# Dilated attention heads of an encoder layer: values two tiles later, and values, transposes and scores in that order within a step

## The chip, the cores and the metric

The kernel runs on one core of one Trainium2 chip. Its metric is the device time of one execution in microseconds (us). A core has five engines that work side by side, each through its own list of instructions in order: TensorE (PE in the profile; its weight loads, which can overlap its matmuls, are listed as PEld), VectorE (DVE), ScalarE (ACT), GpSimd (POOL) and SyncE (SP), which here only issues transfers (DMAs). Engines wait for one another by semaphores. TensorE writes into PSUM, which is cut into banks of 512 float32 values for each of 128 partitions; VectorE and ScalarE read it and write SBUF.

## What is computed

One encoder layer with two attention branches, gates, and an MLP, for a sample of 1024 positions and a prompt of 256. The part that the change touches is the second branch, twelve heads in three groups with dilations 1, 4 and 16:

```python
B_GROUPS = ((128, 1), (512, 4), (2048, 16))
B_HEADS_PER_GROUP = 4

def _dilated_mixture(q, k, v, bias_b):
    for gi, (window, dil) in enumerate(B_GROUPS):
        o, lse = _banded_attention(_to_residues(q[:, :, hs], dil), _to_residues(k[:, :, hs], dil),
                                   _to_residues(v[:, :, hs], dil), window // (2 * dil), dil,
                                   bias_b[:, hs], None)
        ...
    alpha = jax.nn.softmax(jnp.stack(lses), axis=0)
    o = jnp.sum(alpha[..., None] * jnp.stack(outs).astype(jnp.float32), axis=0)
```

Within a head: scores q k^T plus a bias, a maximum over the row, the exponential, its sum, and the product with v. The rest of the layer is `h = rmsnorm(x)`, `z = h @ w_in`, gated sums of the two branches, and `x + square(relu(h @ w_up)) @ w_down`.

## The kernel before

Positions lie in ten tiles of 128. The kernel goes through stages: values of v and the norm; the product with `w_in` in 14 pairs of column blocks; the windowed heads with the remaining gate columns; the merge and `w_out`; the MLP. Each float32 product is made from three products of rounded parts (`hi`, `lo`), and the large ones by a scheme that trades one of eight block products for sums; so each weight block is split on ScalarE (`hi`, L316) and VectorE (`lo`, L318) before use.

The dilated heads run inside the product with `w_in`, in the last five column pairs (`MIXED` = 9 to 13). `pair` (L950) makes one pair with blocks of dense matmuls (`seven`, `prompt`) and calls `tick` (L1015) in the middle of each block and after it. Every second tick advances the generator `attention_b` (L482) by one step. So a step of the heads lands in the middle of each dense block, and twelve dense matmuls of 512 columns (or twenty-four of 256) stand between two steps on TensorE. The schedule is written by hand: the program's order is each engine's order.

`tick` also calls `flush` (L858), which issues stores of gate columns (`scr_g`) on SyncE that were queued two or more ticks before, ahead of the step of that tick. With the last five pairs `right_pair` (L374) issues its two weight loads (512 KB each, `raw`) on SyncE once in a pair, after the block `S2`, and then advances a split by one operation at a time: ScalarE's part, VectorE's part, and the sums of the block scheme on VectorE.

`attention_b` has 60 tiles of two heads each: for each of two pairs of heads, ten tiles of group 2, ten of group 1 and ten of group 0. A *flat* tile has 128 keys (W = 128), a *band* tile 256 keys, a *split* tile two halves of 64 queries with 128 keys each. Group 2 is flat; group 1 alternates band and split, then has two flat ones; group 0 has seven bands, a split, a band and a split. A step handles tiles j and j + 1 for even j:

- `load_v(j)` (L503): v of a tile from DRAM on SyncE, 64 KB for each block of 128 keys, four buffers.
- `load(j)` (L491): q and k of a tile on SyncE (`qk`, four buffers), and at the first tile of a group its bias on GpSimd.
- `scores(j)` (L512): score matmuls of tiles j and j + 1 into two `sc` banks, one for each head, then on VectorE the sum with the bias into `s` with the row maximum (L533) and its negative into `o` (L535). A head has 64 values, so these matmuls use 64 of the 128 rows. A float32 matmul here is two instructions.
- `exponentials(j)` (L538): two exponentials on ScalarE, in place in `s`.
- `transposes(j, eng)` (L546): two or four transposes of `s` into a `pt` bank (two of these), and a copy by `eng` into the tile's half of `turned_s`.
- `values_of(j, eng, pv)` (L558): value matmuls into the tile's quarter of the `pv` bank (one buffer), a copy by `eng` into `o`, and the store of `o` on GpSimd's queue.

In step j these stand in this order, which is the one each engine's list gets: `load_v` of j - 1 and j; scores of j and j + 1; `load` of j + 4 and j + 5; transposes of j - 2 (copied by ScalarE); values of j - 3 (copied by ScalarE); exponentials of j and j + 1; transposes of j - 1 (copied by VectorE); values of j - 2 (copied by VectorE). So an even tile's values follow its own transposes within a step, and an odd tile's follow in the next. There are 32 steps.

Of the kernel before, what the change touches and what calls it, by code (L numbers as in the profile page):

```python
# [15 lines left out]
P = 128  # L16
# [6 lines left out]
HD = 64  # L23
# [6 lines left out]
ROW = 2 * HD + 4  # L30
# [67 lines left out]
def encoder_kernel(  # L98
# [5 lines left out]
    nc = tc.nc  # L104
# [31 lines left out]
    def bank(tag, name=None):  # L136
        return psum.tile([P, 512], F32, name=name or tag, tag=tag, bufs={"mm": 3, "sc": 2, "pt": 2, "pv": 1}[tag])
# [130 lines left out]
    def moved(eng, out, in_):  # L268

        if eng is nc.scalar:  # L270
            nc.scalar.activation(out, in_, AF.Copy)  # L271
        else:
            nc.vector.tensor_copy(out, in_)
# [208 lines left out]
    def attention_b(make):  # L482
# [3 lines left out]
        order = [(g, i, t, tile) for i in range(2) for g in (2, 1, 0) for t, tile in enumerate(_group_tiles(g))]  # L486
        n = len(order)
        held, live, bias = {}, {}, {}
# [14 lines left out]
        def load_v(j):  # L503
            if not 0 <= j < n:
                return
            g, i, t, (pieces, W, _) = order[j]
            v = held[j][1] = make("v", (P, 2, P), n=4)
            for a, (_, _, _, ka) in enumerate(pieces):
                for k in range(W // P):
                    nc.sync.dma_start(v[:, a + k, :], values_rows(g, i, ka // P + k))  # L510

        def scores(j):  # L512

            banks = [bank("sc") for _ in range(2)]
            at = lambda k, h: banks[h][:, 2 * P * (k - j) : 2 * P * (k - j) + order[k][3][1]]
            for k in (j, j + 1):
                g, i, t, (pieces, W, c0) = order[k]
                qk = held[k][0]
                for h in range(2):
                    rows = HALVES[h]  # L520
                    for a, (p0, nq, _, _) in enumerate(pieces):
                        nc.tensor.matmul(at(k, h)[p0 : p0 + nq, :], qk[rows, p0 : p0 + nq],  # L522
                                         qk[rows, P + P * a : P + P * a + W], start=True, stop=True,
                                         skip_group_check=True)
            for k in (j, j + 1):
                g, i, t, (pieces, W, c0) = order[k]
                whole, *flat = bias[g, i]
                b = whole[:, :, c0 : c0 + W] if c0 is not None else flat[pieces[0][2] >= NS]
                s = make("s", (P, 2, 2 * P), n=4)
                m = small.tile([P, 2], F32, name="m", tag="m")  # L530
                o = make("o", (P, ROW), n=5)
                for h in range(2):
                    nc.vector.tensor_tensor_reduce(s[:, h, :W], at(k, h), b[:, h, :], 1.0, -3.0e38,  # L533
                                                   op0=ALU.add, op1=ALU.max, accum_out=m[:, h : h + 1])
                nc.vector.tensor_scalar(o[:, 2 * HD : 2 * HD + 2], m, -1.0, None, op0=ALU.mult)  # L535
                live[k] = s, o
# [18 lines left out]
            moved(eng, pt[:, :a, :], ps[:, : P * a].rearrange("p (i q) -> p i q", q=P))  # L555
            live[j] = pt, o

        def values_of(j, eng, whole):  # L558

            if not 0 <= j < n:  # L560
                return
            g, i, t, (pieces, W, _) = order[j]
            (pt, o), (_, v) = live.pop(j), held.pop(j)
            pv = whole[:, P * (j % 2) : P * (j % 2) + P]
            for h in range(2):
                for a, (p0, nq, _, _) in enumerate(pieces):
                    for k in range(W // P):
                        nc.tensor.matmul(pv[p0 : p0 + nq, HD * h : HD * h + HD], pt[:, 2 * k + h, p0 : p0 + nq],  # L568
                                         v[:, a + k, HALVES[h]], start=k == 0, stop=k == W // P - 1,
                                         skip_group_check=True)  # L570
            moved(eng, o[:, : 2 * HD], pv)
            for p0, nq, qa, _ in pieces:
                nc.gpsimd.dma_start(scr_b[g][qa : qa + nq, i, :], o[p0 : p0 + nq, :])

# [4 lines left out]
        load(3)  # L579
        yield  # L580
        yield
        for j in range(0, n + 3, 2):
            load_v(j - 1)
            load_v(j)
            if j < n:
                scores(j)
            load(j + 4)
            load(j + 5)
            pv = bank("pv") if j else None
            if 0 < j <= n:  # L590
                transposes(j - 2, nc.scalar)
            values_of(j - 3, nc.scalar, pv)
            if j < n:
                exponentials(j)
                exponentials(j + 1)
            if 0 < j <= n:
                transposes(j - 1, nc.vector)
            values_of(j - 2, nc.vector, pv)
            yield

    def entering():
# [443 lines left out]
    if True:  # L1045
# [11 lines left out]
        live, units = {}, {}  # L1057
# [139 lines left out]
    if True:  # L1197
# [61 lines left out]
        order = [(u, t) for u in range(4) for t in range(NT)]  # L1259
        n = len(order)  # L1260
# [277 lines left out]
    class Down:  # L1538
# [4 lines left out]
        def make(self, name, shape=(P, 2, 512), dt=F32):  # L1543
            return self.late.tile(list(shape), dt, name=name, tag="l4", bufs=8)
# [334 lines left out]
```

## Time and profile before

| | us |
|---|---|
| time, median of 3 runs | 1748.45 |
| lowest and highest run | 1746.77, 1752.15 |
| span of the profiled execution | 1745.6 |
| first scores of the dilated heads, after the start of the span | 358.5 |
| last values of the dilated heads | 543.4 |

The profile is of one execution; the page gives the span of that execution and no time of its own beside it, so what lies around the span isn't seen apart from the runs: their median is 2.85 us above the span. A row of a list in order of time has the start, the duration, the engine, the line of the kernel, the operation, the result and its inputs, the shape and a count; `[0.38 <-ACT o L271]` behind it says that the engine sat idle for 0.38 us before it and that ScalarE's instruction on `o` at line 271 released it. Where the engine that is named had long been done, the true releaser is another one, often a transfer. A row with a count above one stands for several instructions in a run. The end of a matmul is modelled: matmuls overlap, so the distance between two starts says more than a duration. SPq rows are issues of transfers on SyncE; the list of transfers gives for each kind its size and the time from issue to landing.

### The profile page before, as it was taken

What the parts mean: (1) busy time and instruction counts of PE and PEld (TensorE: products, weight loads), DVE (VectorE), ACT (ScalarE), POOL (GpSimd) and SP (SyncE); (2) the same over time, 40 slices, a digit from 0 to 9 for tenths busy, and PEclk for the clock granted to TensorE, in tenths of its full rate; (3) what the DMA queues carried; (4) which work ended last, traced back from release to release, by engine and by line L of the source; (5) the groups of instructions that cost most, each with busy time, mean ns of one, the idle gap of its engine ahead of it and who ended that gap; (6) DMA issues with size and microseconds to landing.
All of it is one profiled execution on the core that took longest, in us unless ns stands there. A gap on an engine that the chain in (4) does not pass through costs nothing.

```text
span 1745.6 us, 25270 instructions
## 1 busy us (share of the span) xinstructions
PE 1713.3 (98%) x9248; PEld 1453.1 (83%) x9248; DVE 976.1 (56%) x1708; ACT 725.4 (42%) x1528; POOL 521.0 (30%) x452
## 2 busy tenths in 40 slices
PE   7999999999999999999999999999999999999998
PEld 6898888877778899988888788888888788888886
DVE  6732323445553566676558645454546776657575
ACT  6232222355553455654346433333333333333344
POOL 0212222212221344200000255555655442304050
PEclk9999999999999999999999999999999999999999
DMA  6414343566555753476212243344336844633333
GB/s 235 143 43 151 101 135 115 143 189 174 166 156 151 216 169 82 125 273 219 71 48 97 85 154 124 118 144 154 124 123 239 296 160 151 217 115 115 115 115 121
DMA packets 214780, 256.36 MB, mean 147 GB/s; under 512 B 24887, under 2 KB 144523, under 8 KB 214528
## 3 DMA queue, kind: packets, MB, share of 16 engines
q1 hardware_dynamic: 201424, 228.26, 40.5%
q0 software_dynamic: 12144, 24.38, 4.6%
q10 hardware_dynamic: 1088, 2.10, 0.3%
q8 instruction: 73, 1.20, 0.3%
q14 instruction: 51, 0.42, 0.1%
HBM read 169.10 MB, written 90.73 MB: 149 GB/s over the span
## 4 chain that ended last, share of the span: by engine, by line
PE 88%; DVE 4%; ACT 3%; DMA 2%; issue 2%; POOL 1%; SPq 0%; ACTq 0%; DVEq 0%; POOLq 0%
PE dn L351 20%; PE x L351 17%; PE mm L192 13%; PE z L351 9%; PE v L735 5%; PE pv L351 5%; PE mm L351 4%; PE y L351 4%; PE pv L1104 2%; PE pv L568 2%; PE sc L522 1%; PE pt L1091 1%; PE pt L553 1%; PE tr L342 1%; PE sc L1067 1%
## 5 line engine op out<-in xcount | busy, mean ns | idle before, releaser
L351 PE MATMUL dn<-dhi,ulo 128*128 128x512 f32 x448 | 174.6, 390 | 2.7 <-DVE ulo L186 2.7
L351 PE MATMUL dn<-dhi,uhi 128*128 128x512 f32 x448 | 174.3, 389 | 0.0
L351 PE MATMUL dn<-dlo,uhi 128*128 128x512 f32 x448 | 174.3, 389 | 0.0
L351 PE MATMUL x<-chi,wlo 128*128 128x512 f32 x424 | 167.3, 394 | 2.1 <-DVE u L1752 1.4
L351 PE MATMUL x<-clo,whi 128*128 128x512 f32 x424 | 165.7, 391 | 0.1
L351 PE MATMUL x<-chi,whi 128*128 128x512 f32 x424 | 165.1, 389 | 0.0
L318 DVE TENSOR_TENSOR wlo<-ta,whi 128x1024 fp32r<-128x1024 f32 x30 | 55.8, 1858 | 178.4 <-ACT whi L316 178.4
L318 DVE TENSOR_TENSOR wlo<-raw,whi 128x1024 fp32r<-128x1024 f32 x60 | 90.7, 1512 | 95.3 <-ACT whi L316 95.3
L393 POOL TENSOR_TENSOR tb<-raw 128x512 f32<-128x512 f32 x25 | 33.7, 1347 | 362.6 <-PE mm L192 137.6
L351 PEld LDWEIGHTS dn<-dhi,ulo 128*128 128x128 f32 x448 | 84.1, 188 | 21.3 <-DVE ulo L186 3.8
L186 DVE TENSOR_TENSOR ulo<-uraw,uhi 128x1024 fp32r<-128x1024 f32 x56 | 92.9, 1679 | 11.7 <-ACT uhi L185 11.7
L351 PEld LDWEIGHTS dn<-dhi,uhi 128*128 128x128 f32 x448 | 84.1, 188 | 17.5
L351 PEld LDWEIGHTS dn<-dlo,uhi 128*128 128x128 f32 x448 | 84.1, 188 | 17.3
L351 PEld LDWEIGHTS x<-chi,wlo 128*128 128x128 f32 x424 | 79.8, 188 | 18.4 <-issue 1.8
L351 PEld LDWEIGHTS x<-chi,whi 128*128 128x128 f32 x424 | 79.6, 188 | 17.1
L351 PEld LDWEIGHTS x<-clo,whi 128*128 128x128 f32 x424 | 79.8, 188 | 14.9 <-DVE clo L318 0.4
L1577 POOL TENSOR_TENSOR t<-raw,t 128x1024 f32<-128x1024 f32 x16 | 47.8, 3007 | 141.2 <-DMA raw<-in_w_down_dram 141.2
L1728 DVE TENSOR_TENSOR v<-v,dn 128x512 f32<-128x512 f32 x90 | 59.5, 682 | 42.9 <-PE dn L351 38.2
L271 ACT ACTIVATE pt<-pt 128x512 f32<-128x512 f32 (+1 forms) x70 | 39.1, 558 | 91.0 <-PE pt L553 71.7
L1824 POOL TENSOR_TENSOR u<-u,u 128x640 f32<-128x640 f32 x16 | 25.6, 1597 | 163.2 <-ACT u L1749 163.2
L351 PE MATMUL pv<-phi,wlo 128*128 128x256 f32 x256 | 72.5, 283 | 1.7 <-ACT u L1748 1.7
L351 PE MATMUL dn<-dhi,up 128*128 128x512 f32 x224 | 73.5, 389 | 0.0
(337 smaller groups left out, 4801.4 us busy)
## 6 DMA issues: line engine op xcount, KB each, us to landing
scr_u<-u SPq DMA_DIRECT2D x112, 320.0 KB, 2.6
uraw<-scr_u SPq DMA_DIRECT2D x56, 512.0 KB, 4.3
raw<-in_w_in_dram SPq DMA_DIRECT2D x33, 512.0 KB, 5.9
raw<-in_w_up_dram SPq DMA_DIRECT2D x32, 512.0 KB, 5.3
raw<-in_w_down_dram SPq DMA_DIRECT2D x28, 512.0 KB, 6.7
sg<-scr_g SPq DMA_DIRECT2D x32, 256.0 KB, 5.1
uraw<-scr_u SPq DMA_DIRECT2D x28, 256.0 KB, 4.6
v<-scr_v SPq DMA_DIRECT2D x96, 64.0 KB, 2.4
```

What stands on the lines that cost most here:

```text
L186: nc.vector.tensor_tensor(lo, src, hi.bitcast(F32), op=ALU.subtract)
L192: nc.tensor.matmul(ps, a, b, start=i == 0, stop=i == len(seq) - 1)
L271: nc.scalar.activation(out, in_, AF.Copy)
L318: nc.vector.tensor_tensor(lo, src, hi.bitcast(F32), op=ALU.subtract)
L351: nc.tensor.matmul(ps, a, b, start=first and i == 0, stop=last and i == len(seq) - 1, skip_group_check=True)
L393: (nc.vector if vector else nc.gpsimd).tensor_tensor(o, x, y, op=ALU.subtract)
L568: nc.tensor.matmul(pv[p0 : p0 + nq, HD * h : HD * h + HD], pt[:, 2 * k + h, p0 : p0 + nq], v[:, a + k, HALVES[h]], start=k == 0, stop=k == ...
L735: nc.tensor.matmul(ps[:, :n], a, b, start=k == 0 and j == 0, stop=k == KC - 1 and j == 2)
L1104: nc.tensor.matmul(pv[:, HD * h : HD * h + HD], pt[:, 2 * b + h, :], src, start=b == 0, stop=b == W // P - 1)
L1577: nc.gpsimd.tensor_tensor(o, a, b, op=ALU.subtract)
L1728: nc.vector.tensor_tensor(v, v, ps, op=ALU.add)
L1824: nc.gpsimd.tensor_tensor(u[S1], u21, u22, op=ALU.add)
```

## The change

Within a step the order becomes: `load_v` of j - 2 and j - 1; values of j - 4 and j - 3, one behind the other into the `pv` bank; their copies (ScalarE, VectorE) and stores; transposes of j - 2 and j - 1, each with its copy; scores of j and j + 1; `load` of j + 4 and j + 5; exponentials. The copy and the store leave `values_of` for a new function, `store_values`. An even tile's values thus come a whole step after its transposes, as the odd tile's do. `s` gets two buffers instead of four, `o` eight instead of five. The range of steps runs to n + 4 instead of n + 3, which is 32 steps in both.

```diff
--- before.py
+++ after.py
@@ -526,9 +526,9 @@
                 g, i, t, (pieces, W, c0) = order[k]
                 whole, *flat = bias[g, i]
                 b = whole[:, :, c0 : c0 + W] if c0 is not None else flat[pieces[0][2] >= NS]
-                s = make("s", (P, 2, 2 * P), n=4)
+                s = make("s", (P, 2, 2 * P), n=2)
                 m = small.tile([P, 2], F32, name="m", tag="m")
-                o = make("o", (P, ROW), n=5)
+                o = make("o", (P, ROW), n=8)
                 for h in range(2):
                     nc.vector.tensor_tensor_reduce(s[:, h, :W], at(k, h), b[:, h, :], 1.0, -3.0e38,
                                                    op0=ALU.add, op1=ALU.max, accum_out=m[:, h : h + 1])
@@ -555,12 +555,10 @@
             moved(eng, pt[:, :a, :], ps[:, : P * a].rearrange("p (i q) -> p i q", q=P))
             live[j] = pt, o
 
-        def values_of(j, eng, whole):
-
-            if not 0 <= j < n:
-                return
-            g, i, t, (pieces, W, _) = order[j]
-            (pt, o), (_, v) = live.pop(j), held.pop(j)
+        def values_of(j, whole):
+
+            _, _, _, (pieces, W, _) = order[j]
+            pt, v = live[j][0], held.pop(j)[1]
             pv = whole[:, P * (j % 2) : P * (j % 2) + P]
             for h in range(2):
                 for a, (p0, nq, _, _) in enumerate(pieces):
@@ -568,7 +566,11 @@
                         nc.tensor.matmul(pv[p0 : p0 + nq, HD * h : HD * h + HD], pt[:, 2 * k + h, p0 : p0 + nq],
                                          v[:, a + k, HALVES[h]], start=k == 0, stop=k == W // P - 1,
                                          skip_group_check=True)
-            moved(eng, o[:, : 2 * HD], pv)
+
+        def store_values(j, eng, whole):
+            g, i, _, (pieces, _, _) = order[j]
+            o = live.pop(j)[1]
+            moved(eng, o[:, : 2 * HD], whole[:, P * (j % 2) : P * (j % 2) + P])
             for p0, nq, qa, _ in pieces:
                 nc.gpsimd.dma_start(scr_b[g][qa : qa + nq, i, :], o[p0 : p0 + nq, :])
 
@@ -579,23 +581,25 @@
         load(3)
         yield
         yield
-        for j in range(0, n + 3, 2):
+        for j in range(0, n + 4, 2):
+            load_v(j - 2)
             load_v(j - 1)
-            load_v(j)
+            if j > 2:
+                pv = bank("pv")
+                values_of(j - 4, pv)
+                values_of(j - 3, pv)
+                store_values(j - 4, nc.scalar, pv)
+                store_values(j - 3, nc.vector, pv)
+            if 0 < j <= n:
+                transposes(j - 2, nc.scalar)
+                transposes(j - 1, nc.vector)
             if j < n:
                 scores(j)
             load(j + 4)
             load(j + 5)
-            pv = bank("pv") if j else None
-            if 0 < j <= n:
-                transposes(j - 2, nc.scalar)
-            values_of(j - 3, nc.scalar, pv)
             if j < n:
                 exponentials(j)
                 exponentials(j + 1)
-            if 0 < j <= n:
-                transposes(j - 1, nc.vector)
-            values_of(j - 2, nc.vector, pv)
             yield
 
     def entering():
```

## Prediction

> **What bounds the kernel now.** I read the page first, then the busy times by stage, then the waits of the stage that the change touches, then single steps of it in order of time.
>
> ```profile
> span 1745.6 us, 25270 instructions
> ...
> PE 88%; DVE 4%; ACT 3%; DMA 2%; issue 2%; POOL 1%; SPq 0%; ACTq 0%; DVEq 0%; POOLq 0%
> ```
>
> TensorE (PE) carries 88% of the chain that ended last. So a change is worth what it takes from TensorE's own time: cycles between two matmuls in which it has nothing to do. The dilated heads lie in one stage, from the first scores to the last values:
>
> ```profile
> 358.00:545.00 187.00, 182.94 (x1295) 142.70 (x1294) 97.41 (x400) 97.75 (x334) 44.65 (x80) 1.00 0.59 165
> ```
>
> The columns are the stretch, its length, then busy us of PE, PE's weight loads, VectorE, ScalarE and GpSimd, the granted clock, the DMA share and GB/s. PE's modelled busy time hides short waits, since the modelled ends overlap; VectorE and ScalarE are at 52% each (97.4 and 97.8 of 187), so neither is the bound. The clock is 1.00 throughout. The waits of the weight loads in this stage (total us, times, longest) show the thing that the change aims at:
>
> ```profile
> PEld pv L568 <- ACT o L271: 10.1, 29, 0.5
> ...
> PEld pv L568 <- DVE m L533: 1.7, 8, 0.5
> ```
>
> 29 of the 30 steps that have an even tile's values wait there for ScalarE's copy of the odd tile's values out of the same PSUM bank. One step in order of time, with two flat tiles (W = 128), shows it:
>
> ```profile
> 463.08 0.39 PE L351 MATMUL x<-clo,whi 128*128 128x512 f32 x1
> ...
> 463.31 0.39 PE L351 MATMUL x<-chi,whi 128*128 128x512 f32 x1
> ...
> 463.63 0.71 PE L522 MATMUL sc<-qk 64*128 64x128 f32 x8
> ...
> 464.28 0.44 PE L553 MATMUL pt<-ident,s 128*128 128x128 f32 x2
> ...
> 464.38 0.29 DVE L533 CUSTOM_DVE_ANT_0 s<-sc,bias 128x128 f32<-128x128 f32 x1 [0.51 <-PE sc L522]
> ...
> 464.55 0.56 PE L568 MATMUL pv<-v,pt 128*128 128x64 f32 x4
> ...
> 464.95 0.39 PE L553 MATMUL pt<-ident,s 128*128 128x128 f32 x2
> ...
> 465.15 0.28 ACT L271 ACTIVATE o<-pv 128x128 f32<-128x128 f32 x1
> ...
> 465.32 0.39 ACT L543 ACTIVATE s<-s,o 128x128 f32<-128x128 f32 x1
> ...
> 465.47 0.52 PEld L568 LDWEIGHTS pv<-v,pt 128*128 128x128 f32 x4 [0.38 <-ACT o L271]
> ...
> 465.94 0.48 PE L351 MATMUL x<-chi,wlo 128*128 128x512 f32 x1
> ...
> 466.47 0.39 ACT L543 ACTIVATE s<-s,o 128x128 f32<-128x128 f32 x1
> ```
>
> Dense matmuls start every 0.23 us (463.08, 463.31), so the last one is through at 463.54, and the next dense one starts at 465.94: the step costs PE 2.40 us. In it, eight score instructions take 0.65 (463.63 to 464.28), two transposes 0.27, four value matmuls 0.40 (464.55 to 464.95), two transposes about 0.24. That ends at 465.19, but the even tile's values start at 465.47, 0.04 after the copy into o ends (465.15 + 0.28). PE has lost 0.28 us.
>
> **The change, part by part.** Edits are costed on PE's time line.
>
> *1. The wait that goes.* The same reading for a step with a band and a split tile, and for one with two bands:
>
> ```profile
> 448.59 0.44 PE L553 MATMUL pt<-ident,s 128*128 128x128 f32 x2
> 449.19 1.10 PE L568 MATMUL pv<-v,pt 128*128 128x64 f32 x8 [0.17 <-ACT o L271]
> ```
>
> ```profile
> 428.20 1.00 PE L568 MATMUL pv<-v,pt 128*128 128x64 f32 x8
> 429.04 0.61 PE L553 MATMUL pt<-ident,s 128*128 128x128 f32 x4
> 429.57 1.10 PE L568 MATMUL pv<-v,pt 128*128 128x64 f32 x8
> ```
>
> Band and split: two transposes from 448.59 end at about 448.83, values at 449.19: 0.36 lost; such steps differ a little by which tile is the split one, and I take 0.34. Two bands: four transposes (0.49) from 429.04 end at 429.53, values at 429.57: 0.04. The tiling gives 12 flat, 12 band-and-split and 6 band steps: 12 x 0.28 + 12 x 0.34 + 6 x 0.04 = 7.7 us. After the change the values of a step have their transposed probabilities from the step before, and both tiles' values precede both copies, so this wait has no cause left. So does a wait at 368.42 (row in part 4), the longest of the second row of waits, 0.5: there the odd tile's values wait for their v load, and the new order has that wait in part 4. Together **-8.2 us**.
>
> *2. Where the array changes shape.* Scores use 64 of the 128 rows, and their weight loads don't run ahead: 463.31 + 0.23 to 463.63 is 0.09 lost on entering. On leaving:
>
> ```profile
> 359.12 0.50 PE L351 MATMUL x<-chi,wlo 128*128 128x512 f32 x1
> 359.46 0.39 PE L351 MATMUL x<-clo,whi 128*128 128x512 f32 x1
> ```
>
> 0.34 instead of 0.23 to the next dense matmul, 0.11 lost. Now scores are entered from the dense matmuls and left for transposes; after, they are entered from transposes and left for dense ones: still one way in, one way out. The other new border, dense to a full-row float32 instruction, is in the last step, which has no scores:
>
> ```profile
> 537.36 0.40 PE L351 MATMUL z<-hhi,whi 128*128 128x512 f32 x1
> ...
> 537.60 0.60 PE L553 MATMUL pt<-ident,s 128*128 128x128 f32 x4
> ```
>
> 0.24 apart: nothing lost. So 0, within 0.1 us a step either way (30 steps: -3 to +3).
>
> *3. What becomes late: the exponentials.* The reductions wait for a bank that both tiles' scores fill: the first starts at 464.38, 0.10 after the last score instruction, and the first exponential 0.94 later (465.32). After the change the scores are PE's last work of the step, so with T the return to dense matmuls the last exponential ends near T + 0.1 + 0.7 + 1.54 = T + 2.35, against T + 0.92 now (466.47 + 0.39 against 465.94). Their reader, the next transposes, comes after twelve dense matmuls (2.77) and the values (0.80): T + 3.57. Covered by 1.2 us. For two bands an exponential takes 0.50:
>
> ```profile
> 429.41 0.50 ACT L543 ACTIVATE s<-s,o 128x256 f32<-128x256 f32 x1
> ```
>
> Four of them end near T + 3.0, and the values ahead of the transposes take 1.7 (two times 0.84, 428.20 to 429.04): again 1.4 to spare. Cost 0; without this cover it would be about 1 us a step. The copies move ahead of the reductions on VectorE and of the exponentials on ScalarE, where they wait for PE work that is earlier in the step. Weight splits and evacuations queue behind the exponentials and come 1.4 us later; their readers on PE are a whole block of twelve matmuls and a step away, over 4 us.
>
> *4. What becomes late: the v loads.* This is the cost. Values now open a step: the loads that they need are wanted about 1.3 us earlier (scores 0.65, transposes 0.27, the switch 0.2, and the saving), and SyncE, which issues everything in order, holds its qk loads until the scores that free their buffers, now the last PE work: 0.9 us later in a flat step. Behind those stand the raw weight loads, and behind these the v loads. In order of issue, with the landing of the first v behind each pair of weight loads and PE's first values:
>
> ```profile
> 362.07 0.71 PE L522 MATMUL sc<-qk 64*128 64x128 f32 x8
> ```
>
> ```profile
> 360.84 1.15 SPq L381 DMA_DIRECT2D raw<-in_w_in_dram  x2
> 362.04 2.82 SPq L510 DMA_DIRECT2D v<-scr_v  x2
> ```
>
> ```profile
> v<-scr_v SPq DMA_DIRECT2D x1, 64.0 KB, 6.2
> ```
>
> ```profile
> 368.42 0.63 PE L568 MATMUL pv<-v,pt 128*128 128x64 f32 x4 [0.30 <-DVE m L533]
> ```
>
> ```profile
> 464.33 0.38 SPq L498 DMA_DIRECT2D qk<-scr_qb  x1
> ...
> 467.23 1.08 SPq L381 DMA_DIRECT2D raw<-in_w_in_dram  x2
> 468.41 2.35 SPq L510 DMA_DIRECT2D v<-scr_v  x2
> ```
>
> ```profile
> v<-scr_v SPq DMA_DIRECT2D x1, 64.0 KB, 6.0
> ```
>
> ```profile
> DMA to landing us min/median/max: 1.8/2.4/6.2
> ```
>
> A v load takes 2.4 us in the median but 6.2 and 6.0 behind weight loads. *Tiles 0 and 1:* both v loads will stand where the row at 362.04 stands and land from 368.24 on. PE: the step at j = 2 begins at 361.98 (0.09 before 362.07), transposes 0.49, switches 0.2, scores 0.65, dense 2.77: ready at 366.1. It waits 2.1. *Tiles 36 and 37:* the step at j = 36 is the one shown; its dense matmuls end at 463.54, by the saving of the step before at 463.26. PE leaves it at 463.26 + 0.80 + 0.49 + 0.65 + 0.2 = 465.4; qk loads begin at 465.2 instead of 464.33, so the v load is issued at 469.3 instead of 468.41 and lands 6.0 later, at 475.3. PE gets there after dense 2.77, a step of 2.14 and dense 2.77, at 473.1. It waits 2.2. The same working at the two other weight loads, ahead of tiles 18 and 54, gives 0.2 and 0, because band tiles lengthen the steps between.
>
> *5. Gate stores ahead of v loads.* SyncE also waits for a gate sum that VectorE makes behind a weight split:
>
> ```profile
> 458.49 0.68 DVE L927 TENSOR_TENSOR z<-y,c 128x512 f32<-128x512 f32 x1
> ```
>
> ```profile
> 459.20 0.32 SPq L860 DMA_DIRECT2D scr_g<-z  x1
> 459.62 0.88 SPq L510 DMA_DIRECT2D v<-scr_v  x2
> ```
>
> Since the split follows the exponentials, all this slides by 1.4 us: the store to 460.6, the two v loads to 461.0 and 461.5, landing (2.4) by 463.9. Tile 33's values are wanted at 463.26 + 0.40 = 463.7. Some 0.2 to 0.5 here; the places like it are the one-in-nine steps after a split in four column pairs, and the same slide gives 0.4, 0.4, 0.2 and 0.1 at those that matter. Parts 4 and 5 sum to 2.1 + 2.2 + 0.2 + 1.1 = 5.6; bounds: 0 if every v lands in 1.8, and 14 if each of the 24 steps that are not two bands waits 0.4 besides the two long ones.
>
> *6. The rest at nothing.* GpSimd: the stores of o now precede the bias loads of the same step; they wait for copies at most 2 us, and a bias is wanted two steps (about 10 us) later. s with 2 buffers: transposes that free them precede the scores on PE. o with 8: six are live, two are on their way out; that is as much room as now. v and qk keep 4. The number of steps stays 32; the last one gets two tiles' values instead of one, the step at j = 2 loses one.
>
> Sum: -8.2 + 0 + 5.6 = **-2.6 us**. The profiled span is 1745.6, 2.85 under the median of 1748.45; against the median this gives 1745.8.
>
> A sentence beside this from the Trainium skill, *DMA: Bandwidth & Descriptors*, section "Queues, rings and completion order": descriptors of a ring are consumed in ring order; the 6.2 against 2.4 us agrees. By that page's "Specifications" (about 358 GB/s of HBM for a core) the 1.05 MB of two weight loads would take 2.9 us, an estimate, after which v would land near 366 at the first place instead of 368.24; both long waits would be gone and the sum would be about -7. The measured landings decide.
>
> **Rivals.**
>
> *The v loads are never late* (SyncE or the rings have more room than the two rows say). For it: the median of 2.4 us, and most steps have 2 us to spare by the working of part 4. Against it: 368.42, where the present order already waits for a v. Then -8.2: 1740.2.
>
> *The v loads become the bound (slower).* Place: SyncE's queue, where qk loads now wait for the end of the step's PE work, so that each v load starts a step's length behind it. Price: in a flat step v is issued near T + 3.2 and wanted at T + 2.77 + 2.14 + 2.77 = T + 7.7; a landing after more than 4.5 us stalls PE one for one. It decides from 8.2 us of waits in all, 0.27 a step. With 14 us, +5.8: 1754.3. For it: landings of 5 to 6 us in four places; against: they are four.
>
> *The change doesn't do what it says:* the values still wait for a copy, since there is one values bank (pv) and the next step's values need both copies of the last. Against it: those copies are issued before exponentials and are over 2 us old by then. Then 0 + 5.6: 1754.
>
> **How the numbers follow.** The forecast, part of the gain eaten by late v loads, gets 0.50, with its own range 1743 to 1749; never late 0.27; v the bound 0.17; wait stays 0.06. A measurement of this kernel can tell about 0.3%, 5.2 us, from no change, so the forecast itself counts as the same. Faster by more: the 0.27 and 0.04 of the forecast's fast edge, 0.31. Slower by more: most of the two slow rivals, 0.19. Same: 0.50. The range leaves a tenth out on each side: 1739 to 1756.5.
>
> **What would show it.** Right: no wait of pv for o on ScalarE; flat steps of 4.9 instead of 5.2 us; pv waiting for v at tiles 0 and 36 for about 2 us; exponentials ending 2.3 us into the dense matmuls with no wait of the transposes. Wrong: transposes waiting for s (part 3), values waiting for v in most steps, or a gap between scores and dense matmuls above 0.11 (part 2).

## The result, and the profile after

The kernel got slower by 0.28%: 1752.82 us in the median after (1749.2 to 1758.89, 20 runs) against 1747.91 before (1746.48 to 1752.15, 20 runs); the ratio is 1.0028 with a 95% interval of 1.002 to 1.0036. That is 4.9 us, a little less than the 5.2 us that the prediction took as the least it could tell from no change; with 20 runs of each the interval still lies clear of 1. The forecast was 1745.8.

First the page's head and its chain of waits:

```profile
span 1751.8 us, 25171 instructions
...
PE 85%; DVE 5%; DMA 4%; ACT 3%; issue 2%; SPq 1%; POOL 1%; DVEq 0%; ACTq 0%; POOLq 0%
```

The profiled span is 6.2 us longer than before (1751.8 against 1745.6), and 4% of the chain is now DMA, 2% before. The stage of the dilated heads, as before by busy us of PE, its weight loads, VectorE, ScalarE and GpSimd, granted clock, DMA share and GB/s:

```profile
358.00:549.00 191.00, 182.34 (x1294) 149.00 (x1293) 95.39 (x398) 99.50 (x334) 43.78 (x79) 0.97 0.57 162
```

The granted clock is 0.97 where it was 1.00. The first dense matmul behind the stage starts at 547.55 instead of 543.35, and the first scores of the windowed heads follow at 578.60 instead of 574.39: of these 4.2 us, 3.9 are lost in this stage and 0.3 ahead of it. The other 2 us lie behind it: a copy that splits a raw weight (at 594.05, before at 588.53) waits 1.7 us for its load instead of 0.4, and the remaining 0.6 us was not followed up.

The waits of the stage, of PE and of its weight loads (total us, times, longest):

```profile
PE pv L566 <- DMA v<-scr_v: 8.3, 6, 3.5
```

```profile
PEld pv L566 <- issue: 9.0, 6, 3.9
```

The row with ScalarE's copy of o (10.1 us, 29 times) is gone, and no row of the transposes waiting for s has come. In their place PE waits six times for v, 8.3 us in all, once 3.5. These six lie in five steps (j = 4, 18, 28, 40 and 58); shorter waits for v in four others stand under another engine's name or in no row of their own. A row counts from the modelled end of the last dense matmul; by the distance between starts a wait is some 0.16 us longer, and the text below goes by that unless it quotes a row. The second row is the weight loads' side of the same waits: what stands in front of them waits, and they with it. VectorE has a large new row, for which PE doesn't wait:

```profile
DVE o L273 <- ACT o L271: 49.0, 19, 7.4
```

The second tile's copy waits for the first one, which reads the same bank. An undisturbed flat step (the one at j = 8) in order of time, on PE and then on ScalarE:

```profile
377.48 0.39 PE L351 MATMUL x<-chi,whi 128*128 128x512 f32 x1
377.70 1.00 PE L566 MATMUL pv<-v,pt 128*128 128x64 f32 x8
378.54 0.61 PE L553 MATMUL pt<-ident,s 128*128 128x128 f32 x4
379.08 0.71 PE L522 MATMUL sc<-qk 64*128 64x128 f32 x8
379.72 0.50 PE L351 MATMUL x<-chi,wlo 128*128 128x512 f32 x1
```

```profile
378.74 0.28 ACT L271 ACTIVATE o<-pv 128x128 f32<-128x128 f32 x1 [0.39 <-PE pv L566]
...
381.44 0.40 ACT L543 ACTIVATE s<-s,o 128x128 f32<-128x128 f32 x1 [2.09 <-DVE o L535]
...
382.62 0.39 ACT L543 ACTIVATE s<-s,o 128x128 f32<-128x128 f32 x1
```

From 377.71 (the last dense matmul's start and 0.23) to 379.72 the step costs PE 2.01 us, 0.39 less than the flat step shown of before. The last exponential ends at 383.01, 3.3 us into the dense work, and nothing waits for it. And the worst step, at j = 40, whose values need tiles 36 and 37; SyncE's issues first, then the time to landing of that v load, then PE:

```profile
463.24 0.32 SPq L864 DMA_DIRECT2D scr_g<-z  x1
...
464.62 0.39 SPq L498 DMA_DIRECT2D qk<-scr_qb  x1
...
467.44 1.38 SPq L381 DMA_DIRECT2D raw<-in_w_in_dram  x2
468.87 2.42 SPq L510 DMA_DIRECT2D v<-scr_v  x1
```

```profile
v<-scr_v SPq DMA_DIRECT2D x1, 64.0 KB, 6.4
```

```profile
471.47 0.39 PE L351 MATMUL x<-chi,whi 128*128 128x512 f32 x1
475.39 1.94 PE L566 MATMUL pv<-v,pt 128*128 128x64 f32 x8 [3.53 <-DMA v<-scr_v]
...
478.11 1.86 PE L522 MATMUL sc<-qk 64*128 64x256 f32 x12
479.90 0.79 PE L351 MATMUL x<-chi,wlo 128*128 128x512 f32 x1
```

The v load is issued at 468.87 behind 1.05 MB of raw weights and lands 6.4 us later, at 475.27; PE has been ready since 471.70. What the wait costs doesn't end there: eight value matmuls take 1.94 us instead of 1.00, and the scores 1.86 instead of about 1.08 for the same twelve. The same view by windows shows why (the column before the last two is the granted clock):

```profile
473.00:474.00 1.00, 0.00 (x0) 0.00 (x0) 0.00 (x0) 0.00 (x0) 0.00 (x0) 0.90 1.11 309
474.00:475.00 1.00, 0.00 (x0) 0.00 (x0) 0.00 (x0) 0.00 (x0) 0.00 (x0) 0.50 0.82 227
475.00:480.00 5.00, 4.61 (x25) 3.33 (x25) 0.71 (x2) 0.66 (x2) 1.07 (x2) 0.50 0.28 81
480.00:481.00 1.00, 1.00 (x3) 0.84 (x4) 0.93 (x6) 0.00 (x0) 0.00 (x0) 0.69 0.31 81
...
535.00:536.00 1.00, 1.00 (x8) 1.00 (x8) 0.02 (x1) 0.28 (x1) 0.00 (x0) 0.62 0.00 0
536.00:538.00 2.00, 2.00 (x10) 1.02 (x8) 0.69 (x2) 0.60 (x1) 1.07 (x2) 0.50 0.18 63
538.00:539.00 1.00, 1.00 (x12) 0.62 (x11) 0.24 (x1) 0.00 (x0) 0.00 (x0) 0.68 0.03 9
```

A mean of 0.90 over a microsecond is a fifth of it at a half: the clock falls at 473.8, 2.1 us after PE ran dry, and is back at 480.6. At j = 58, whose values begin at 533.53 after 1.87 us without work, it falls too, 1.7 us after PE has begun again, and for 3.4 us.

How the steps of the two kernels and of the experiments compare, in us of PE from the end of the dense matmuls (start of the last and 0.23) to the next dense one, read from the timeline as in the flat step. A step is named by the tiles of its scores; its values are those of earlier ones. The last row sums the 32 steps of the stage:

| step | before | after | v earlier | copies last | weights on ScalarE | gate stores behind | values in same step | copy between |
|---|---|---|---|---|---|---|---|---|
| j = 8, flat | 2.39 | 2.01 | 2.01 | 2.11 | 2.01 | 2.02 | 2.87 | 2.60 |
| j = 14, band and split | 3.59 | 3.12 | 3.13 | 3.42 | 3.12 | 3.13 | 3.17 | 4.02 |
| j = 24, two bands | 3.93 | 3.76 | 3.77 | 3.74 | 3.77 | 3.77 | 3.84 | 4.34 |
| j = 4 | 2.94 | 3.66 | 2.02 | 2.12 | 2.02 | 4.53 | 2.09 | 2.60 |
| j = 18 | 3.22 | 4.31 | 2.76 | 3.05 | 4.11 | 2.76 | 2.80 | 3.39 |
| j = 40 | 2.76 | 8.20 | 2.38 | 3.63 | 5.03 | 8.94 | 2.45 | 2.96 |
| j = 58 | 3.88 | 6.97 | 3.50 | 3.48 | 4.56 | 4.52 | 3.17 | 4.08 |
| all 32 | 95.4 | 98.3 | 83.5 | 89.6 | 92.2 | 95.5 | 88.2 (31 steps) | 101.4 |

### The profile page after: what moved, and what is told of

It reads as the page before. It is cut to its first block, busy times and chain, and to the rows that moved or that the text cites. A ratio compares the mean times of both kernels' runs of the same rounds, so it can differ in the third digit from the quotient of the medians.

```text
span 1751.8 us, 25171 instructions
## 1 busy us (share of the span) xinstructions
PE 1713.2 (98%) x9248; PEld 1459.5 (83%) x9248; DVE 976.2 (56%) x1708; ACT 727.1 (42%) x1528; POOL 518.8 (30%) x452
## 4 chain that ended last, share of the span: by engine, by line
PE 85%; DVE 5%; DMA 4%; ACT 3%; issue 2%; SPq 1%; POOL 1%; DVEq 0%; ACTq 0%; POOLq 0%
PE dn L351 20%; PE x L351 17%; PE mm L192 13%; PE z L351 8%; PE v L739 5%; PE pv L351 5%; PE y L351 4%; PE mm L351 4%; PE pv L1108 2%; PE pv L566 2%; DMA v<-scr_v 1%; PE sc L522 1%; PE pt L1095 1%; PE pt L553 1%; PE tr L342 1%
## 5 line engine op out<-in xcount | busy, mean ns | idle before, releaser
L351 PEld LDWEIGHTS x<-clo,whi 128*128 128x128 f32 x424 | 79.9, 189 | 14.8 <-DVE clo L318 0.4
L543 ACT ACTIVATE s<-s,o 128x128 f32<-128x128 f32 (+1 forms) x120 | 51.9, 434 | 52.3 <-DVE o L535 48.3
```

Of the source, the lines that this page charges most:

```text
L351: nc.tensor.matmul(ps, a, b, start=first and i == 0, stop=last and i == len(seq) - 1, skip_group_check=True)
L543: nc.scalar.activation(s[:, h, :W], s[:, h, :W], AF.Exp, bias=nm[:, h : h + 1], accum_out=l[:, h : h + 1])
```

## The experiments

The theory after the result: the new order by itself saves some 12 us of PE, more than forecast; late v loads and the clock that falls behind them take back some 15. All kernels below but the last were timed in the same rounds as the kernel before, whose median was 1747.98 beside the first four and 1748.07 beside the next three (23 runs each).

**v two tiles earlier.** The changed kernel, with each v load issued a step sooner and room for it:

```diff
-            v = held[j][1] = make("v", (P, 2, P), n=4)
+            v = held[j][1] = make("v", (P, 2, P), n=6)
...
-            load_v(j - 2)
-            load_v(j - 1)
+            load_v(j)
+            load_v(j + 1)
```

> The changed kernel with each v load issued one step earlier (six v buffers). Theory: the new order is worth about 8 us and gives them back through values that wait for v (1.8, 3.6 and 1.7 us at tiles 0, 36 and 54, 2.2 at two others) and through the half clock that follows the two waits of tiles 36 and 54 (about 4 us). Then nothing of this is left: no wait of pv for v, clock 1.00 throughout, about 1740 us, 0.9955 of the kernel before. Rival: the order costs by itself (copies out of one bank one after the other, exponentials late); then pv doesn't wait for v any more and the time is still 1747 or more.

Measured: 1737.52 us (1735.55 to 1738.98, 5 runs), ratio to before 0.9938 (0.9926 to 0.995). No row of PE waiting for v is left, and in the stage, which now ends at 532.58, the clock is 1.00 again (window to 534):

```profile
358.00:534.00 176.00, 176.00 (x1295) 146.33 (x1294) 94.79 (x398) 99.65 (x335) 43.76 (x79) 1.00 0.63 176
```

At j = 40 the values follow the dense matmuls at once:

```profile
466.51 0.39 PE L351 MATMUL x<-chi,whi 128*128 128x512 f32 x1
466.74 1.00 PE L566 MATMUL pv<-v,pt 128*128 128x64 f32 x8
```

Nothing but the place and the room of the v loads differs, and 15.3 us come back (1752.82 to 1737.52), 14.8 of them in the steps (98.3 to 83.5). So the late v loads are the whole of the loss, and this kernel is faster than both. The old order with earlier v loads was not run; its trace has one wait for v to give back, the one at 368.42, of at most 0.5 us. The nine steps that differ by over 0.2 us are those at j = 40 (5.8), 58 (3.5), 4 (1.6), 18 (1.6) and j = 10, 12, 28, 36, 54 (2.2 together).

**Raw weights on ScalarE's queue.** In the column pairs beside the dilated heads, ScalarE issues the raw weight loads instead of SyncE:

```diff
-            nc.sync.dma_start(raw[i], cols[i])
+            (nc.scalar if now[0] is not None and vector else nc.sync).dma_start(raw[i], cols[i])
```

> The changed kernel with the two weight loads of a pair issued on ScalarE's queue in this stage. Theory: v lands 6 us after its issue because it queues behind 1 MB of weights on the same rings; then it lands in about 3, the waits at tiles 0, 36 and 54 fall below 1 us each, the clock stays at 1.00, and the time is 1743 to 1746 us. Rival: SyncE issues v too late because it waits for the scores; then landings are short but these waits stay above 1.5 us, about 1750 to 1752. Second rival: the transfers share the same 16 engines whatever the queue, v still takes 5 to 6 us, and the time stays near 1752.

Measured: 1749.11 us (1745.82 to 1753.87, 12 runs), ratio 1.0007 (0.9997 to 1.0016), 3.7 us under the changed kernel, where 7 to 10 were expected. The step at j = 4 is at 2.02 and the one at j = 58 has lost 2.4 us, so these waits came from the raw weights issued ahead of v. At j = 40 PE is idle for 1.8 us, from 470.48, where its dense matmuls end, to 472.28. The time to landing of that v load, then PE:

```profile
v<-scr_v SPq DMA_DIRECT2D x1, 64.0 KB, 6.0
```

```profile
472.28 1.08 PE L568 MATMUL pv<-v,pt 128*128 128x64 f32 x8 [1.64 <-ACT s L545]
```

The load is issued at 466.18 instead of 468.87, and no raw weights stand ahead of it on SyncE. It still takes 6.0 us and lands at 472.14, right before the values start. The row names ScalarE's exponential, but that one belongs to tiles which these values don't read, and their own transposed tiles were copied by 470.1. So v was issued earlier and did not land faster: at this step the second rival is right, that v takes 5 to 6 us whatever the queue. The clock isn't 1.00 throughout either: it falls to 0.50 from 473.8 to 477.2. The waits that come from gate stores (j = 18: 4.11) are left.

In the profiled execution the stage is 5.8 us shorter than the changed kernel's (183.3 against 189.1), and 4.1 us are lost again behind it, where a copy waits 2.7 us for a raw weight (589.11) and the clock falls from 593.2 to 600.1. ScalarE also stands idle for 2.85 us, by the row for a qk load, with its own issue of a raw weight load (468.75) at the end of it:

```profile
468.75 0.38 ACTq L383 DMA_DIRECT2D raw<-in_w_in_dram  x1
469.17 0.28 ACT L271 ACTIVATE o<-pv 128x128 f32<-128x128 f32 x1 [2.85 <-DMA qk<-scr_qb]
```

PE doesn't wait for that copy here, so what the issues on ScalarE cost is not shown.

**Copies last, alone.** The kernel before with its own order, but both tiles' values ahead of both copies (the first copy goes from between the two values to behind the second):

```diff
-            moved(eng, o[:, : 2 * HD], pv)
...
             values_of(j - 2, pv)
+            store_values(j - 3, nc.scalar, pv)
+            store_values(j - 2, nc.vector, pv)
```

> The kernel before in its old order of PE's work, with one thing of the change: both tiles' values precede both copies. Theory: this alone takes away the wait of the even tile's values for the copy of the odd tile's, about 0.25 us in 24 steps, and leaves the v loads as they were: 1741 to 1743 us. Rival: the even tile's values then wait nearly as long for their own transposed tile, which ScalarE copies in the same step (it ends 0.3 us before the copy of o): about 1747.

Measured: 1742.51 us (1741.63 to 1742.59, 5 runs), ratio 0.9968 (0.9956 to 0.998). The steps fall by 5.8 us in all, the flat one by 0.28, which is the gap that was read in the trace of before; the largest wait left of the values is the one for a copy of the transposes (total us, times, longest):

```profile
PEld pv L568 <- ACT pt L271: 3.3, 12, 0.5
```

At j = 40 the step has grown, from 2.76 to 3.63: PE, ahead of its old time, comes before v there even without the later values.

**Idle time filled.** The changed kernel with 14, 28 and 14 transposes of the identity, whose result nothing reads, ahead of the values at j = 4, 40 and 58. They keep PE busy while v is on its way:

```diff
+FILL = {4: 14, 40: 28, 58: 14}
...
+                if j in FILL:
+                    for a in range(FILL[j]):
+                        nc.tensor.transpose(pv[:, 2 * P : 3 * P], ident, ident)
```

> The changed kernel with transposes of the identity matrix (results not used) put on PE ahead of the values of the steps at j = 4, 40 and 58: 14, 28 and 14 of them, 0.12 us each, which fit into the waits that stand there. Theory: PE isn't idle long, the clock stays at 1.00 where it fell to 0.5, and about 4 us come back though PE has more to do: 1748 to 1749.5 us. Rival: the low clock costs nothing or comes from something else; 1752 to 1753 us, or more if the transposes don't fit.

Measured: 1749.77 us (1748.48 to 1755.34, 11 runs), ratio 1.0018 (1.0009 to 1.0028); 3.0 us under the changed kernel in the median, with ratios whose intervals overlap, and 5.1 us in the profiled span (1746.7).

```profile
465.00:485.00 20.00, 19.60 (x144) 16.02 (x142) 8.13 (x40) 8.83 (x35) 5.54 (x10) 1.00 0.73 204
```

```profile
473.56 3.22 PE L593 MATMUL pv<-ident 128*128 128x128 f32 x28
477.18 1.08 PE L568 MATMUL pv<-v,pt 128*128 128x64 f32 x8 [0.40 <-DMA v<-scr_v]
```

v still comes late (0.40 us idle even behind the filling, which ends at 476.78), but the clock is 1.00, the eight value matmuls take 1.08 us instead of 1.94, and the step at j = 40 costs 6.08 instead of 8.20, the one at j = 58 5.06 instead of 6.97. PE does more in these two steps and is done with them sooner. Of the two steps' loss against the kernel with early v (5.8 and 3.5 us), 2.1 and 1.9 come back with the clock. The stage as a whole is only 1.4 us shorter (187.7 against 189.1): v came later at other steps in this execution, and those at j = 4, where v lands 6.5 us behind its issue instead of 5.5, and at j = 22 are 1.0 us longer each. The other 3.7 us of the span lie outside the stage and are not shown to come from the filling.

**Gate stores behind the step's loads.** The changed kernel, with the two lines of each tick exchanged:

```diff
             ticks[0] += 1
-            flush()
             n = ticks[0] - 18 * MIXED
             if n > 0 and n % 2:
                 next(att_b, None)
+            flush()
```

> The changed kernel, but at each tick SyncE issues the step's own loads first and the stored gate lines behind them. My theory: the extra time of the steps j = 10, 12, 18, 28, 36 and 54 (0.51 + 0.46 + 1.55 + 0.63 + 0.29 + 0.29 = 3.7 us over the same steps with v loaded two tiles earlier) is the gate store, which holds the v load behind it on SyncE. So those steps fall to within 0.1 us of the kernel with the early v loads, the three long waits (j = 4, 40, 58), which are behind the raw weights, stay or shrink by at most 0.4 us each, and the time is 1752.8 less 3.7 to 4.9, about 1748 to 1749. Rival one: the six steps are late because PE comes earlier than any v load can land, whatever lies ahead of it; they stay, and the time stays at 1752 to 1753. Rival two: putting the gate stores behind only moves the wait to the gate's own buffers; then dense work waits for the store of its gate line and the time is 1752 or more, with a new wait row of ScalarE or VectorE for a store.

Measured: 1750.84 us (1746.43 to 1759.22, 12 runs), ratio 1.0019 (1.0006 to 1.0033). The six steps did as expected: those at j = 10, 12, 18, 28, 36 and 54 are within 0.01 us of the kernel with early v, 3.7 us less. But only 2.0 us arrived in the median, and the intervals of the two ratios overlap, since the stores now stand elsewhere: the steps at j = 4, 22 and 40 grew by 0.9, 1.8 and 0.7 us. The long waits were expected to stay or to shrink by at most 0.4 us; instead these two of them grew, and the step at j = 58 fell by 2.5 us, with no fall of the clock behind it. Behind j = 4 the clock now falls, from 369.0 to 372.4, mostly in dense matmuls between two steps. At j = 40, SyncE, the landing and PE:

```profile
465.86 0.38 SPq L864 DMA_DIRECT2D scr_g<-z  x1
466.28 1.36 SPq L381 DMA_DIRECT2D raw<-in_w_in_dram  x2
467.69 2.77 SPq L510 DMA_DIRECT2D v<-scr_v  x1
```

```profile
v<-scr_v SPq DMA_DIRECT2D x1, 64.0 KB, 7.5
```

```profile
475.34 1.94 PE L566 MATMUL pv<-v,pt 128*128 128x64 f32 x8 [4.26 <-DMA v<-scr_v]
```

The store of a gate is now issued right ahead of the raw weights, and v lands 7.5 us behind its issue instead of 6.4. Neither rival held: the six waits did come from the store, and no dense work waits for one; but what is taken off one v load lies in front of another.

**Values in the same step.** The kernel with early v, without the longer lag: transposes of two tiles, scores of the next two, then values of the same two tiles as the transposes (v loaded two steps ahead):

```diff
-            if j > 2:
-                pv = bank("pv")
-                values_of(j - 4, pv)
-                values_of(j - 3, pv)
...
             if j < n:
                 scores(j)
             load(j + 4)
             load(j + 5)
+            if j:
+                pv = bank("pv")
+                values_of(j - 2, pv)
+                values_of(j - 1, pv)
```

> The kernel with the early v loads, without the part 'values two tiles later': each step does the transposes of the two tiles before, then the scores of the next two, then the values of the same two tiles whose transposes have just been made, with both tiles' values ahead of both copies, and v loaded two steps ahead. Theory one: with transposes ahead of scores, the scores (0.6 us of a flat step, 1.1 us of one with a band) cover the two copies of the transposes (0.4 to 0.6 us each), so the longer lag of the values buys nothing but its own wait for v: 1737 to 1739, steps within 0.1 us of 2.0 flat and 3.1 mixed. Theory two: the copies start late, because ScalarE and VectorE still work on the dense part (0.57 and 0.69 us each) when the transposes end, and the lag is what hides this: each of the 32 steps gets longer by 0.2 to 0.5 us, 1744 to 1753, with wait rows of the values for copies of pt on ScalarE and VectorE of 6 us or more together.

Measured: 1745.23 us (1742.39 to 1748.2, 11 runs), ratio 0.9982 (0.9973 to 0.9992), 7.7 us above the kernel with early v. Most flat steps are 0.1 us longer, but the one at j = 8 by 0.86; VectorE and PE there:

```profile
377.23 1.23 DVE L318 TENSOR_TENSOR wlo<-raw,whi 128x1024 fp32r<-128x1024 f32 x1 [2.19 <-ACT whi L316]
378.38 0.68 DVE L933 TENSOR_TENSOR z<-z,c 128x512 f32<-128x512 f32 x1
378.98 0.42 DVE L273 COPY pt<-pt 128x256 f32<-128x256 f32 x1
```

```profile
378.22 0.66 PE L566 MATMUL pv<-v,pt 128*128 128x64 f32 x4
379.45 0.66 PE L566 MATMUL pv<-v,pt 128*128 128x64 f32 x4 [0.56 <-DVE pt L273]
```

The scores do cover the copies (theory one) wherever ScalarE and VectorE are free, which is in most steps; in a few the copy of the transposes stands behind 1.9 us of dense work on VectorE (theory two), and PE waits 0.56. The time lies in the range of theory two, but partly by luck: only 3.9 of the profile's 6.4 us (1742.2 against 1735.8) lie in the stage. The other 2.5 came behind it, where PE waits 2.8 us for VectorE up to 743.87 instead of 1.3 us and the clock is at a half from 743.7 to 747.1; why that wait is longer was not followed up.

**A copy between the values.** The kernel with early v, but the first tile's copy back between the two tiles' values:

```diff
                 values_of(j - 4, pv)
-                values_of(j - 3, pv)
                 store_values(j - 4, nc.scalar, pv)
+                values_of(j - 3, pv)
                 store_values(j - 3, nc.vector, pv)
```

> The kernel with the early v loads, but the first tile's copy is put back between the two tiles' values, as in the kernel before; the values stay two tiles later and the transposes ahead of the scores. My theory: the second tile's values wait for ScalarE's copy out of the same bank in each of the 32 steps, 0.28 to 0.34 us as in the kernel before (8.2 to 11 us in all): 1745.5 to 1748.5, a wait row of the values for ScalarE's copy of o with some 30 entries, and PE waits of about 0.3 us a step. Rival: the values are now the first work of a step, and the gain of the other parts is what made the 10 us; then it stays at 1737 to 1740.

Measured: 1755.45 us (1754.1 to 1759.55, 5 runs), ratio 1.0047 (1.0034 to 1.006): 17.9 us above the kernel with early v, twice what was expected.

```profile
PEld pv L566 <- ACT o L271: 17.3, 30, 1.1
```

```profile
376.91 1.04 ACT L316 ACTIVATE whi<-raw 128x1024 fp32r<-128x1024 f32 x1
377.86 0.25 ACT L271 ACTIVATE o<-pv 128x128 f32<-128x128 f32 x1
```

```profile
377.24 0.55 PE L566 MATMUL pv<-v,pt 128*128 128x64 f32 x4
378.16 0.66 PE L566 MATMUL pv<-v,pt 128*128 128x64 f32 x4 [0.37 <-ACT o L271]
```

The wait is there in 30 steps, and longer than it was in the kernel before (17.3 us against 10.1). The values now open the step, when ScalarE is still at dense work: here a weight split of 1.04 us stands ahead of the copy, of which PE waits for the end. In the order of before, scores and transposes lay between. So the later values and the transposes ahead, without the copies at the end, lose.

**The changed kernel again,** unaltered:

> The changed kernel once more, unaltered, for a second profile. If the long waits and the lower granted clock belong to the kernel and not to one execution, the values at j = 40 wait again for v by 3 to 4 us and those at j = 58 by 1.5 to 2.5 us, the granted clock is 0.5 to 0.7 for some us after each, and the stage ends (first scores of the windowed heads) at 578 to 579 us. The 1.3 us by which a copy of the next stage waited longer for its raw weights near 590 us may or may not come again: if it is part of the change it does, at 1 to 1.5 us.

Measured, one run: 1756.92 us, beside 1746.8 for the kernel before. The first scores of the windowed heads start at 582.16, later than in the first profile (578.60) and than expected. The waits are the same in kind, and in more places:

```profile
PE pv L566 <- DMA v<-scr_v: 9.1, 8, 3.5
```

```profile
409.00:410.00 1.00, 0.54 (x7) 0.42 (x7) 0.28 (x1) 0.00 (x0) 0.00 (x0) 0.80 0.78 214
...
478.00:481.00 3.00, 3.00 (x16) 2.50 (x15) 0.72 (x2) 0.66 (x2) 0.86 (x2) 0.50 0.28 72
```

The step at j = 40 costs 8.02 again and the one at j = 58 6.46. This time the one at j = 18 takes 5.79 instead of 4.31: two shorter waits there, of 0.26 and 0.97 us, are enough for the clock to fall. The copy behind the stage waits for its raw weight again (1.6 us); with early v it is 0.5, and in the changed kernel with filled waits it is gone, so what brings it is not shown. How late v comes differs from one execution to the next, and the whole difference of the two profiled spans (3.3 us) lies in this stage. That fits the spread of the times, which no trace explains run by run: 9.7 us over the 20 runs of the changed kernel, 5.7 over those of the kernel before, 3.4 over the 5 with early v.

## Why the prediction was wrong

The direction was wrong. The gain was put at 8.2 us and is 11.9; the late loads were put at 5.6 and cost 14.8, waits and clock together. 1752.82 lies inside the whole range (1739 to 1756.5), which the slow rivals had widened, and outside the forecast's own, 1743 to 1749. Each step by itself:

*Part 1, the wait that goes (-8.2).* The wait is gone as forecast, and the size was off: copies last alone, which takes away only this wait, saves 5.8 us in the steps (95.4 to 89.6), and the whole order with v in time 11.9 (95.4 to 83.5). The flat step's 0.28 is what copies last alone brings (2.39 to 2.11). Band and split was put at 0.34 and is 0.46: 0.17 from the copies, and 0.29 from the rest of the order, for in the old order the gap that the copy leaves is filled by another wait, for the copy of the transposes (the row of 3.3 us in 12 steps, 0.28 each). Values in the same step, with the scores between transposes and values, are at 3.17 and so have most of these 0.29 without the later values. Two bands were put at 0.04 and are 0.16, all of it from the copies.

*Part 2, the array's shape (0, within 0.1 a step).* Flat steps get shorter by another 0.10 (2.11 to 2.01) with no wait left in either kernel, so the border is the likely cause: from transposes to scores PE goes on at once (378.54 to 379.08 is four transposes), where dense to scores lost 0.09. That is 1.2 us in 12 steps, inside the bounds; two-band steps don't show it, and the shape was not varied alone.

*Part 3, exponentials later (0).* Right, but with less room than forecast: the first starts 1.7 us into the dense work (381.44 against 379.72), not 0.8, the last ends at 3.3 instead of 2.35, and of 1.2 us of cover some 0.3 is left. No transpose waits for s.

*Part 4, late v loads (4.5), is the step that failed*, together with part 5. The mechanism was right, v behind raw weights, and the sizes were wrong. Tile 0 was put at 2.1 and waits 1.6, and tile 18 at 0.2 and shows none; tile 36 was put at 2.2 and waits 3.7, and tile 54 at 0 and waits 1.9. At tile 36 even the landing came as forecast (475.3), but PE was ready at 471.70, not 473.1: SyncE had kept its time while PE had got ahead of it. I had taken SyncE's start from the qk loads alone, 1.9 us into PE's step at j = 36 (465.2 against 463.26); it is 3.0 us (464.62 against 461.62, where the dense work ahead of that step ends), because the gate store of part 5, issued at 463.24, holds the queue in front of them. With the gate stores behind, they do start 1.9 us into it (463.06 against 461.13). Parts 4 and 5 were costed as if they were two queues: the slide of the store was charged to the v load just behind it, and not to the qk loads, the raw weights and the v load behind these.

*Part 5, gate stores (1.1).* Right in kind, as the exchange of the two lines shows, but 3.7 us in six steps. The slide was put at 1.4 us; against PE's step at j = 36 the store has slid by 2.3, from 0.6 ahead of the end of the dense work (462.90 against 463.54 before) to 1.6 behind it (463.24 against 461.62).

*What had no term.* A wait has a second price: 4.0 us of granted clock. I had read the clock of 1.00 in the trace of before and not asked what an idle PE does to it. With 10.7 us of waits and 4.0 of clock against a gain of 11.9, the steps come out at +2.9 us; the forecast had -8.2 and +5.6. Another 1.0 us lies in the dense work between the steps (0.7 of it with early v too), which was not followed up, and 2.0 behind the stage.

*The rivals.* "The v loads become the bound" gave 1754.3, 1.5 us from the result, for 14 us of waits; the measured waits and clock are 14.8. That it came so near is partly luck, since its gain was 3.7 us too small, its waits left out the clock, and 2 us lie behind the stage. Its place was half right: nine steps, not each one outside two bands, and with the larger gain it decides from 11.9 us, not from 8.2. "Never late" gave 1740.2; made true, it is 1737.5. "Doesn't do what it says" is excluded by the missing wait for o.

*By the Trainium skill* the prediction had an estimate of about -7 from *DMA: Bandwidth & Descriptors*, "Specifications", if the weights moved at the stated bandwidth of a core. The landings of 6.4 and, with a gate store ahead, 7.5 us speak against that bandwidth as a price. They agree with the same page's ring order ("Queues, rings and completion order"), but that is not the whole cause: with the raw weights on ScalarE's queue v still took 6.0 us.

## What to carry to other kernels

When a consumer is moved forward in a loop, move its loads forward by as much: the new order is worth 10.5 us with that edit, and cost 4.9 without it. Work out how late a load comes along its whole queue, with every store, wait and byte ahead of it, and not at one link of it; then add to each wait of TensorE of about 2 us or more what the clock takes behind it. Parts of a reordering may pay only together: of the three here, the copies last alone gave 5.5 us, the two others without them, v early, lost 7.4, and all three with their loads in time gave 10.5.

## What was not expected of the hardware

The granted clock halves after little idle time: 2.1 us into a wait of 3.7 us; after a wait of 1.87 us only 1.7 us past its end, for 3.4 us; in another execution right behind two waits of 0.26 and 0.97 us; not after one of 1.56 us at j = 4. How much idle time it takes is not settled: a wait of 1.8 us was followed by the lower clock (raw weights on ScalarE, j = 40), one of 1.76 us was not (gate stores behind, j = 22). But the moments lie on a grid: by the rows above, the clock of the changed kernel changes at 473.8, 480.6, 535.2 and 538.6, which are 2, 16 and 1 times 3.41 us apart, and in the clock records of all ten profiles every change lies a whole multiple of 3.413 us from the first. So the delay from a wait to the fall depends on where the wait lies on this grid. The Trainium skill, *TensorE: Matmul & The Clock Gate*, "HAM oscillation — how this bites in real kernels", warns of gaps above about 3.4 us; here shorter ones were enough. The window of the Trainium skill, which by the same page ("What's actually happening") is 3413 ns long and runs freely, agrees with the grid, and with the 3.4 and 6.8 us that the lower clock lasted, one window and two.

A DMA issue can hold up the engine that makes it: ScalarE did nothing for 2.85 us up to its issue of a raw weight load. And TensorE was done sooner where its long waits were filled with work that nobody reads: by 2.1 and 1.9 us in the two steps.
